# Gating in the projection's PSUM banks, pooling sums on VectorE, small copies on ScalarE in a two-layer decoder trunk

## The chip, the cores and the metric

The kernel runs on one core of a Trainium2 chip. Its engines are TensorE (PE in the profile, its weight loads apart as PEld), VectorE (DVE), ScalarE (ACT), GpSimd (POOL) and SyncE (SP), which issues the DMA transfers. The metric is the device time of one execution in microseconds; the median over runs counts.

## The reference

One sequence of 512 tokens with 1024 features goes through two layers, each `x <- x + RMSNorm_post(mixer(RMSNorm_pre(x)))`, all in float32. What the change touches lies in layer 0 and in the parameters of layer 1's state-space branch:

```python
def even_mixer(h, w_in, pool_w, pool_scale, w_out):        # layer 0
    z = h @ w_in                                           # 1024 x 3072
    q, k, v, ga, pu, gb = jnp.split(z, [A, 2*A, 3*A, 4*A, 4*A + POOL_WIDTH], axis=-1)   # A = 512
    q, k = rope_partial(q), rope_partial(k)
    att  = moba_attention(q, k, v) * jax.nn.silu(ga)       # 4 heads of 128
    pool = multiscale_pool(pu, pool_w, pool_scale) * jax.nn.silu(gb)   # windows 2, 4, 8, 16
    return jnp.concatenate([att, pool], axis=-1) @ w_out

def multiscale_pool(u, ...):    # group g: mean of the last w_g tokens, minus u, times pool_w[g]
```

Layer 1 does the same with a state-space branch (S5, which needs powers of a complex number per state) and a 31-tap convolution branch with gates.

## The kernel before

**Precision and weights.** A float32 product is made of three matmuls on a high and a low part: `mm3` (lines 104, 105, 106: high by high, then the two cross products). `split` (L107 to L111) makes the parts: ScalarE copies the source into the high part (`S.activation`, L109), and VectorE, or GpSimd where it is told to, subtracts it from the source (`tt`, L58). So all subtractions, additions and products show as L58, scaled ones as L61. Weights come in blocks of 256 rows: SP loads `raw` (three buffers, L146), ScalarE makes `whi` (L109, with a gain L169), and `wlo` is made by VectorE (L61, layer 0's input projection) or by GpSimd (L58, layer 0's output projection and layer 1). `whi` and `wlo` have four buffers each; a block's buffers come free when its last matmul or split is done.

**Stages of layer 0.** After the norm and transposes come the column groups of the input projection, each of four output tiles of 128x512 in the four PSUM banks of pool `pz` (tag `z`): q, k, v, then `pg0` and `pg1` (values and gates of pooling groups 0, 1 and 2, 3), then `ga` (gates of the four attention heads). Attention runs on TensorE between the matmuls of pg0 to ga: scores `s`, weights `P`, their transposes `tp` (L721), the split `ph`, `pl` and the sums `o`. Then the output projection (`out_mm`, order groups `o00` and `o01` for the two halves of the columns) makes eight tiles of 128 tokens by 512 columns; for each it goes through eight blocks of gated branch output, first the four pooling groups (`ch`, `cl`), then the four heads (also in a tile that the profile calls `qk`).

**Pooling.** `pool_branch` makes, for a group, the gate `sgb`, the padded values `u`, and one to four doubling sums `ub` (L802 and the line after it): each clears a strip at the left edge and adds a tile to itself, shifted. `m` (a `wt`) is the mean minus the value. `pool_mm` multiplies by `pool_w` and the gate and splits into `ch` and `cl`.

**Gating of the heads.** After `ga`, VectorE multiplies each of the four banks by `rbc` (the reciprocal norm, along the tokens) into an SBUF tile `sgs[g]`, ScalarE applies Silu in place, VectorE multiplies by the attention output `att` into another SBUF tile `yc`, and `split` makes the two parts. Each bank is free after its first product.

**Side work on GpSimd.** From about 30 to 164 us GpSimd computes for layer 1 the phasors (`U`, `pa`) and the tables (`tab`, two tiles per step, chains of short products on 128x4 to 128x256, stored by SP as `td`, L757). The table tiles share a ring of buffers (tag `ch`) with the pooling groups' `ch` and `cl`. `s5_bc` copies the powers `AR`, `AI` in reversed order into `GR`, `GI` (eight copies of 128x32, L537 and L538), from which VectorE makes `g` (L58).

**What sets the order.** The program is not run in the order of its text: the framework's scheduler simulates it and gives each engine a fixed list of instructions, which that engine executes strictly in order, waiting on semaphores. SP's DMA issues stand in such a list too. An instruction that waits holds back all that stand behind it on its engine.

Of the kernel before, what the change touches and what calls it, by code (L numbers as in the profile page):

```python
# [14 lines left out]
F32 = mybir.dt.float32  # L15
# [3 lines left out]
AF = mybir.ActivationFunctionType  # L19
# [4 lines left out]
MUL, ADD, SUB, MAX, MIN = ALU.mult, ALU.add, ALU.subtract, ALU.max, ALU.min  # L24
# [3 lines left out]
Q = 4  # L28
# [10 lines left out]
def tile_hybrid_trunk(ctx, tc, A):  # L39
    nc = tc.nc  # L40
    x, out = A["x"], A["out"]
    V, S, G = nc.vector, nc.scalar, nc.gpsimd
# [6 lines left out]
    pz = ctx.enter_context(tc.tile_pool(name="pz", bufs=4, space=PSUM))  # L49
# [4 lines left out]
    def f(ap):  # L54
        return ap.bitcast(F32)

    def tt(e, o, a, b, op):
        return e.tensor_tensor(o, a, b, op=op)  # L58
# [10 lines left out]
    def tcol(t):  # L69
        return slice(t * 128, (t + 1) * 128)  # L70
# [37 lines left out]
    def split(hi, lo, src, eng=None):  # L108
        i = S.activation(hi, src, AF.Copy)  # L109
        tt(eng or V, lo, src, f(hi), SUB)  # L110
        return i  # L111
# [85 lines left out]
    def proj_t(name, sh, sl):  # L197

        z = zbanks()
        for j in range(4):  # L200
            w = wblock(name, j)
            for t in range(4):
                for i in range(2):
                    k = j * 2 + i
                    last_mm[0] = mm3(z[t], sh[k][:, tcol(t)], sl[k][:, tcol(t)], w.h[i], w.l[i], k == 0, k == 7).ins
            run_after(name, j)
        return z
# [26 lines left out]
    ps = l0.enter_context(tc.tile_pool(name="ps", bufs=2, space=PSUM))  # L234
# [89 lines left out]
    def wt():  # L324
        return wk.tile([128, 512], F32, tag="t", name="wt", bufs=5)
# [39 lines left out]
    def e2k(tag, bufs=1):  # L365
        return pe.tile([128, 512], F32, tag=tag, name=tag, bufs=bufs)
# [136 lines left out]
    def s5_bc():  # L503
        AR, AI, fr, fi = (par[n] for n in ("AR", "AI", "fr", "fi"))
        ct1 = pe.tile([128, NG, NI], F32, name="ct1")
        ct2 = pe.tile([128, NG, NI], F32, name="ct2")
        p = pt.tile([128, 512], F32, tag="t", name="tp")
        with tc.issue_after(q_end[0]):
            for m in range(4):
                nc.tensor.transpose(p[:, tcol(m)], par["cn"][:, m].rearrange("p a b -> p (a b)"), ident)  # L510
        S.activation(ct1.rearrange("p g c -> p (g c)"), p, AF.Copy, scale=s2)
        S.activation(ct2[0:64].rearrange("p g c -> p (g c)"), p[64:128], AF.Copy)
        S.activation(ct2[64:128].rearrange("p g c -> p (g c)"), p[0:64], AF.Copy, scale=-1.0)
        for g, r in enumerate(DR):
            d = par["dm"][r, :, g * NI:g * NI + NI]
            tt(G, d, d, ident[r, r.start + NI:r.stop].unsqueeze(1).to_broadcast([32, NG // 2, NI]), MUL)
        IC = pe.tile([128, 8, 128 + 2 * NI], F32, name="IC")
        G.tensor_copy(IC[:, :, 0:128], ident.unsqueeze(1).to_broadcast([128, 8, 128]))
        kk = pe.tile([128, NG // 2, 2 * NI], F32, name="kk")


        b1, b2 = par["b1"], par["b2"]

        def bc(ap):
            return ap.unsqueeze(2).to_broadcast([128, NG, NI])
        u1, u2 = (e2k(n, b).rearrange("p (g i) -> p g i", i=NI) for n, b in (("e2", 1), ("pin", 2)))
        tt(V, u1, b2, bc(fi), MUL)
        tt(V, u2, b1, bc(fi), MUL)
        tt(V, b1, b1, bc(fr), MUL)
        tt(V, b2, b2, bc(fr), MUL)  # L530
        tt(V, b1, b1, u1, SUB)
        tt(V, b2, b2, u2, ADD)

        GR = pe.tile([128, Q, NG], F32, name="GR")
        GI = pe.tile([128, Q, NG], F32, name="GI")
        for i in range(Q):
            G.tensor_copy(GR[:, i], AR[:, Q - 1 - i])  # L537
            G.tensor_copy(GI[:, i], AI[:, Q - 1 - i])  # L538
        par.update(ct1=ct1, ct2=ct2, GR=GR, GI=GI, IC=IC, kk=kk)

    def s5_phasors():
# [93 lines left out]
    rbc = wk.tile([128, T], F32, name="rbc", bufs=1)  # L635
# [13 lines left out]
    def q_first():  # L649
        z = zbanks()  # L650
        steps = [("h", 0), ("w", 0), ("h", 1), (0, 0), ("h", 2), (1, 0), ("w", 1), (0, 1), (1, 1), "l", ("h", 3), (2, 0), ("w", 2), ("x", 0), ("x", 1), (2, 1), (3, 0), (3, 1), ("w", 3), ("x", 2), ("x", 3), "s", (0, 2), (1, 2), (2, 2), (3, 2), (0, 3), (1, 3), (2, 3), (3, 3)]
        w = {}
        for st in steps:
            if st == "l":
                s5_lam()
            elif st == "s":
                root0()
                run_after("q", 0)
            elif st[0] == "x":
                ss0(st[1])  # L660
            elif st[0] == "h":
                hT0(st[1])
            elif st[0] == "w":
                w[st[1]] = wblock("q", st[1], 0)
            else:
                t, j = st
                for i in range(2):
                    k = j * 2 + i
                    last_mm[0] = mm3(z[t], h0h[k][:, tcol(t)], h0l[k][:, tcol(t)], w[j].h[i], w[j].l[i], k == 0, k == 7).ins
        q_end[0] = last_mm[0]  # L670
        return z

    qk = []
    for name, nxt in (("q", "k"), ("k", "v")):
        z = q_first() if name == "q" else proj_t(name, h0h, h0l)
# [51 lines left out]
    att = []  # L727
# [36 lines left out]
    z = proj_t("v", h0h, h0l)  # L764
    for t in range(4):
        a = xv.tile([128, 512], F32R, tag="v", name="vh")
        b = xv.tile([128, 512], F32R, tag="v", name="vl")
# [19 lines left out]
    ch, cl = [None] * 8, [None] * 8  # L787
    ms, sgb = {}, {}

    def pool_branch(g, zg, zu):  # L790
        sgb[g] = pu.tile([128, 16 + 512], F32, tag="u", name="sgb", bufs=5)[:, 0:512]
        tt(V, sgb[g], zg, rbc, MUL)
        S.activation(sgb[g], sgb[g], AF.Silu)
        w = 2 << g
        u = pu.tile([128, 16 + 512], F32, tag="u", name="u", bufs=5)
        G.memset(u[:, 0:16], 0.0)
        tt(V, u[:, 16:], zu, rbc, MUL)
        a = u
        step = 1
        while step < w:  # L800
            b = pu.tile([128, 16 + 512], F32, tag="u", name="ub", bufs=5)
            G.memset(b[:, 0:step], 0.0)  # L802
            tt(G if g in (0, 1) else V, b[:, step:], a[:, step:], a[:, :528 - step], ADD)
            a = b
            step *= 2
        m = wt()
        tt(V, m[:, 0:16], a[:, 16:32], rcnt[:, g], MUL)
        tt(V, m[:, 0:16], m[:, 0:16], u[:, 16:32], SUB)
        stt(V, m[:, 16:], a[:, 32:], 1.0 / w, u[:, 32:], MUL, SUB)
        mh = cp.tile([128, 512], F32R, tag="mh", name="mh")  # L810
        ml = cp.tile([128, 512], F32R, tag="ml", name="ml")
        split(mh, ml, m)
        ms[g] = (mh, ml)
# [10 lines left out]
    for n, nxt in ((0, "pg1"), (1, "ga")):  # L824
        z = proj_c(f"pg{n}", h0h, h0l)
        for i in range(2):
            g = 2 * n + i
# [33 lines left out]
    after["ga", 2] += [load_gains]  # L861
    z = proj_c("ga", h0h, h0l)
    cah, cal = bigr(), bigr()
    sgs = [wt() for _ in range(4)]
    for g in range(4):
        tt(V, sgs[g], z[g], rbc, MUL)
        if g == 1:
            pool_mm(3)
        S.activation(sgs[g], sgs[g], AF.Silu)
    for g in range(4):  # L870
        sg = sgs[g]
        yc = wt()
        tt(V, yc, att[0][:, g], sg, MUL)
        ch[g], cl[g] = cah[:, g], cal[:, g]
        split(ch[g], cl[g], yc)


    def out_mm(z, names, c, t, ch, cl, kord, ahead):
# [39 lines left out]

    xns, yg, ss = [], defaultdict(list), defaultdict(list)
    for t, q in ((0, 0), (1, 0), (0, 1), (1, 1), (2, 0), (2, 1), (3, 0), (3, 1)):  # L920
        z = pz.tile([128, 512], F32, tag="z", name="z")
        out_mm(z, f"o0{q}", full, t, ch, cl, OK0, lambda j: 3 if t + q == 0 else 3 - j)
        ss[t].append(sumsq(z, wk))
        yg[t].append(wt())
        tt(V, yg[t][q], z, gpost[q], MUL)
        if (t, q) == (3, 0):
            prefetch(index["sa", 0] + 4)
        if q:
            if t:
                next_hT(t - 1, xns[t - 1])  # L930
            xns.append(add_norm(t, yg[t], ss[t]))
# [12 lines left out]
    ps = l1.enter_context(tc.tile_pool(name="ps1", bufs=1, space=PSUM))  # L944
# [220 lines left out]
    z = proj_c("sb", hh, hl)  # L1165
# [3 lines left out]
    z = proj_c("ab1", hh, hl)  # L1169
    for i in range(2):  # L1170
        conv_in(2 + i, z[i], z[2 + i])
    z = proj_c("gd", hh, hl)
# [8 lines left out]
    z = proj_c("gc", hh, hl)  # L1181
# [13 lines left out]
    ch, cl, sn = [], [], []  # L1195
# [12 lines left out]
    for n in range(2):  # L1208

        with tc.issue_after(ln["mu"]) if n else nullcontext():  # L1210
            z = proj_c(f"gl{n}", yh, yl, nk=4)
        for i in range(2):
            m = 2 * n + i
            s = ct()
            S.activation(s, z[2 + i], AF.Sigmoid, bias=gb[:, 4 + m:5 + m])
            a = ct()
# [5 lines left out]
    ch, cl = by_k((c1[0], c2[0])), by_k((c1[1], c2[1]))  # L1222
# [14 lines left out]
    for m in range(4):  # L1237
        z = (pt.tile([128, 512], F32, tag="t", name="z") if m % 2 else (ps, pa)[m // 2].tile([128, 512], F32, tag=("s", "acc")[m // 2], name="z"))
# [5 lines left out]
        a = ct()  # L1244
# [3 lines left out]
    z = zo  # L1248
# [5 lines left out]
    for t in range(4):  # L1254
# [4 lines left out]
        for c in cols:  # L1259
            z = pz.tile([128, 512], F32, tag="z", name="z")  # L1260
# [42 lines left out]
```

## Time and profile before

| | us |
|---|---|
| median of three runs (lowest, highest) | 463.68 (462.9, 465.01) |
| the profiled execution | 464.39 |
| its span, first to last instruction | 462.6 |
| TensorE busy | 442.1 (96%) |
| TensorE weight loads busy | 362.7 (78%) |
| VectorE busy | 344.2 (74%) |
| GpSimd busy | 251.4 (54%) |
| ScalarE busy | 243.9 (53%) |

The mean granted TensorE clock was 0.987 of full speed (the two levels are 2.4 GHz, written 1.00, and 1.2 GHz, written 0.50; a stretch that holds both shows a value between). A table of busy time by stretch says how much each engine worked there; in a line of the timeline the two numbers are start and duration, and a bracket gives the idle time of that engine before it and who ended it. TensorE is nearly always busy, so its few idle stretches and those at the lower clock are what the table has to be read for.

### The profile page before, as it was taken

The numbers are of one execution on the slowest core, as the hardware profiler recorded it, in microseconds if no ns is written. First come the engines' busy times: TensorE is split into PE (matmuls) and PEld (weight loads), VectorE is DVE, ScalarE is ACT, GpSimd is POOL, SyncE is SP. The second block draws the span as 40 slices with busy tenths as digits, with TensorE's granted clock in tenths as the row PEclk, the third lists the DMA queues.
The fourth block names the chain that finished last, engine by engine and source line by source line (L and its number), as shares of the span: only waits on it lengthen the run. The fifth ranks groups of instructions, "written<-read, shape, count | busy, mean of one in ns | idle before, by whom it ended". The sixth has DMA issues, their size and how long they took to land.

```text
span 462.6 us, 6753 instructions
## 1 busy us (share of the span) xinstructions
PE 442.1 (96%) x2185; PEld 362.7 (78%) x2185; DVE 344.2 (74%) x706; ACT 243.9 (53%) x445; POOL 251.4 (54%) x428
## 2 busy tenths in 40 slices
PE   7999989999999979889999999999999999999994
PEld 5788868888878858678879988877877877788884
DVE  3998698757677475864884579998998898656444
ACT  7655435635847334624764535649866326373431
POOL 1019994019999926650281576668997944430000
PEclk9999999999999979989999999999999999999999
DMA  7974064341332555350045693886343542122013
GB/s 255 236 135 162 25 217 147 114 126 47 132 96 77 136 181 195 118 165 1 1 139 156 184 264 103 240 219 161 93 123 113 150 136 92 47 92 91 0 70 112
DMA packets 62403, 59.58 MB, mean 129 GB/s; under 512 B 20537, under 2 KB 43713, under 8 KB 62368
## 3 DMA queue, kind: packets, MB, share of 16 engines
q1 hardware_dynamic: 62368, 59.16, 43.0%
q8 instruction: 17, 0.28, 0.2%
q14 instruction: 18, 0.15, 0.1%
HBM read 50.62 MB, written 8.52 MB: 128 GB/s over the span
## 4 chain that ended last, share of the span: by engine, by line
PE 66%; POOL 16%; DVE 10%; DMA 3%; issue 2%; ACT 1%; SPq 0%; DVEq 0%; POOLq 0%; ACTq 0%
PE z L105 19%; PE z L104 19%; PE z L106 19%; POOL tab L58 12%; PE s L1000 2%; DVE wt L58 1%; PE y L1035 1%; PE y L1032 1%; POOL U L58 1%; DMA ldt<-o_log_dt 1%; DVE wlo L61 1%; POOL pa L58 1%; DMA qk<-x 1%; DVE qk L58 1%; PE tp L589 1%
## 5 line engine op out<-in xcount | busy, mean ns | idle before, releaser
L58 POOL TENSOR_TENSOR wlo<-raw,whi 128x1024 fp32r<-128x1024 f32 (+2 forms) x50 | 88.4, 1790 | 71.8 <-ACT whi L109 71.8
L105 PE MATMUL z<-hl,whi 128*128 128x512 f32 (+1 forms) x288 | 106.6, 371 | 0.0
L104 PE MATMUL z<-hh,whi 128*128 128x512 f32 (+1 forms) x288 | 106.3, 375 | 0.0
L106 PE MATMUL z<-hh,wlo 128*128 128x512 f32 (+1 forms) x288 | 106.2, 371 | 0.0
L61 DVE SCALAR_TENSOR_TENSOR acc<-gp,dw,acc 128x512 f32<-128x512 f32 x100 | 75.1, 751 | 2.2
L109 ACT ACTIVATE whi<-raw 128x1024 fp32r<-128x1024 f32 (+2 forms) x54 | 45.3, 871 | 37.7 <-PE z L105 19.2
L104 PEld LDWEIGHTS z<-hh,whi 128*128 128x128 f32 x288 | 54.5, 190 | 9.7 <-issue 0.8
L106 PEld LDWEIGHTS z<-hh,wlo 128*128 128x128 f32 x288 | 54.6, 190 | 9.0 <-issue 0.2
L105 PEld LDWEIGHTS z<-hl,whi 128*128 128x128 f32 x288 | 54.8, 190 | 8.8 <-issue 0.3
L61 DVE SCALAR_TENSOR_TENSOR wlo<-raw,gcol,whi 128x512 fp32r<-128x512 f32 x48 | 36.6, 783 | 6.6 <-ACT whi L169 4.8
L169 ACT ACTIVATE whi<-raw,gcol 128x512 fp32r<-128x512 f32 x48 | 32.1, 715 | 15.6 <-PE z L106 7.5
L105 PE MATMUL z<-wlo,hh 128*128 128x512 f32 x96 | 38.3, 401 | 1.6 <-DVE wlo L61 1.5
L104 PE MATMUL z<-whi,hh 128*128 128x512 f32 x96 | 38.1, 405 | 1.1 <-ACT whi L169 1.1
L106 PE MATMUL z<-whi,hl 128*128 128x512 f32 x96 | 37.9, 398 | 0.0
L58 POOL TENSOR_TENSOR tab<-tab,U 128x4 f32<-128x4 f32 (+6 forms) x112 | 36.7, 361 | 0.0
L306 ACT ACTIVATE junk<-z 128x512 bf16<-128x512 f32 (+1 forms) x17 | 9.7, 570 | 30.4 <-PE z L106 30.3
L58 POOL TENSOR_TENSOR tab<-tab 128x4 f32<-128x4 f32 (+6 forms) x56 | 23.5, 439 | 0.0
L105 PEld LDWEIGHTS z<-wlo,hh 128*128 128x128 f32 x96 | 18.2, 189 | 6.2 <-DVE wlo L61 2.7
L104 PEld LDWEIGHTS z<-whi,hh 128*128 128x128 f32 x96 | 18.1, 191 | 5.6 <-ACT whi L169 1.8
L106 PEld LDWEIGHTS z<-whi,hl 128*128 128x128 f32 x96 | 18.2, 190 | 3.4
L58 POOL TENSOR_TENSOR pacc<-pacc,lt 128x512 f32<-128x512 f32 x14 | 18.9, 1354 | 0.2
L58 POOL TENSOR_TENSOR dm<-dm,ident 32x256 f32<-32x256 f32 x2 | 1.5, 750 | 30.8 <-DMA dm<-o_d 30.7
(325 smaller groups left out, 1008.3 us busy)
## 6 DMA issues: line engine op xcount, KB each, us to landing
raw<-e_w_in SPq DMA_DIRECT2D x15, 512.0 KB, 4.0
raw<-e_w_in SPq DMA_DIRECT2D x18, 256.0 KB, 3.6
raw<-e_w_out SPq DMA_DIRECT2D x8, 512.0 KB, 4.6
raw<-o_w_in SPq DMA_DIRECT2D x16, 256.0 KB, 3.5
rot<-td SPq DMA_DIRECT2D x16, 256.0 KB, 5.6
raw<-o_w_in SPq DMA_DIRECT2D x8, 512.0 KB, 3.9
raw<-o_w_out SPq DMA_DIRECT2D x8, 512.0 KB, 3.7
qk<-x SPq DMA_DIRECT2D x8, 256.0 KB, 4.1
```

Source lines behind the costliest of these rows:

```text
L58: return e.tensor_tensor(o, a, b, op=op)
L61: e.scalar_tensor_tensor(o, a, s, b, op0=op0, op1=op1)
L104: nc.tensor.matmul(p, sh, mh, start=start, stop=False)
L105: nc.tensor.matmul(p, sh, ml, start=False, stop=False)
L106: return nc.tensor.matmul(p, sl, mh, start=False, stop=stop)
L109: i = S.activation(hi, src, AF.Copy)
L169: S.activation(hi[:, h], b.raw[:, h], AF.Copy, scale=gc)
L306: S.activation(jk[:, 0:src.shape[-1]], src, AF.Square, scale=1.0 / 32.0, accum_out=ss)
L589: nc.tensor.matmul(p[:, i], ev[:, h + i], IC[:, c % 2 * 4 + h + i], start=True, stop=True)
L1000: nc.tensor.matmul(s[:, i], sets[m][0][hf, i], Ut[m][hf, i], start=True, stop=True)
L1032: nc.tensor.matmul(y[:, r], tb[:, m * 4 + r], Ut[m][:, r], start=True, stop=False)
L1035: nc.tensor.matmul(y[i * 64:i * 64 + 64, r], gt[:, g], xf[i][:, r], start=False, stop=True)
```

## The change

Four edits. The eight copies into `GR` and `GI` go from GpSimd to ScalarE. In `pool_branch` all clearings (four of `u`, ten of `ub`) and the three sums of groups 0 and 1 go from GpSimd to VectorE, where the sums of groups 2 and 3 were already. The gated heads are computed in place in the four PSUM banks of `ga`, so that both products and Silu read and write the bank, and `split` reads it. Two of the output projection's tiles, (0,0) and (1,0), take banks of the scores' pool `ps` (tag `s`, two banks, also used by pooling's `y`) in place of `pz`.

```diff
@@ s5_bc
         for i in range(Q):
-            G.tensor_copy(GR[:, i], AR[:, Q - 1 - i])
-            G.tensor_copy(GI[:, i], AI[:, Q - 1 - i])
+            S.activation(GR[:, i], AR[:, Q - 1 - i], AF.Copy)
+            S.activation(GI[:, i], AI[:, Q - 1 - i], AF.Copy)
@@ pool_branch
-        G.memset(u[:, 0:16], 0.0)
+        V.memset(u[:, 0:16], 0.0)
         tt(V, u[:, 16:], zu, rbc, MUL)
...
-            G.memset(b[:, 0:step], 0.0)
-            tt(G if g in (0, 1) else V, b[:, step:], a[:, step:], a[:, :528 - step], ADD)
+            V.memset(b[:, 0:step], 0.0)
+            tt(V, b[:, step:], a[:, step:], a[:, :528 - step], ADD)
@@ after the projection ga
-    sgs = [wt() for _ in range(4)]
+
     for g in range(4):
-        tt(V, sgs[g], z[g], rbc, MUL)
+        tt(V, z[g], z[g], rbc, MUL)
         if g == 1:
             pool_mm(3)
-        S.activation(sgs[g], sgs[g], AF.Silu)
+        S.activation(z[g], z[g], AF.Silu)
     for g in range(4):
-        sg = sgs[g]
-        yc = wt()
-        tt(V, yc, att[0][:, g], sg, MUL)
+        tt(V, z[g], z[g], att[0][:, g], MUL)
         ch[g], cl[g] = cah[:, g], cal[:, g]
-        split(ch[g], cl[g], yc)
+        split(ch[g], cl[g], z[g])
@@ output projection of layer 0
     for t, q in ((0, 0), (1, 0), (0, 1), (1, 1), (2, 0), (2, 1), (3, 0), (3, 1)):
-        z = pz.tile([128, 512], F32, tag="z", name="z")
+        z = (ps if t < 2 and not q else pz).tile([128, 512], F32, tag="s" if t < 2 and not q else "z", name="z")
```

The scheduler makes new lists from it. The first place is VectorE in the second half of pooling, around the sum for group 2. Numbers in the names tell buffers apart: `ub_2186` and `ub_2189` are sums of this group, `pl_2075` is a low part of attention weights, `cl_2010` a low part of pooling group 0. Before:

```order
L61 SCALAR_TENSOR_TENSOR wt_2007<-y_2003,pscale_1576,sgb_1930 128x512 [waits PE_49]
L58 TENSOR_TENSOR ml_1964<-wt_1959,mh_1963 128x512 [waits Activation_49]
L58 TENSOR_TENSOR ub_2186<-ub_2183 128x526 [waits DVE_49,Pool_49]
L58 TENSOR_TENSOR cl_2010<-wt_2007,ch_2009 128x512 [waits DMAHW6_49,Activation_49]
L58 TENSOR_TENSOR ub_2189<-ub_2186 128x524 [waits DVE_49,Pool_49]
L58 TENSOR_TENSOR pl_2075<-tp_2069,ph_2074 128x512 [waits Activation_49]
```

And of the change:

```order
L61 SCALAR_TENSOR_TENSOR wt_2007<-y_2003,pscale_1576,sgb_1930 128x512 [waits PE_49]
L58 TENSOR_TENSOR ml_1964<-wt_1959,mh_1963 128x512 [waits Activation_49]
L802 MEMSET ub_2186 128x2 [waits DVE_49]
L58 TENSOR_TENSOR ub_2186<-ub_2183 128x526
L58 TENSOR_TENSOR cl_2010<-wt_2007,ch_2009 128x512 [waits DMAHW6_49,Activation_49,Pool_49]
L802 MEMSET ub_2189 128x4 [waits DVE_49]
L58 TENSOR_TENSOR ub_2189<-ub_2186 128x524
L58 TENSOR_TENSOR pl_2075<-tp_2069,ph_2074 128x512 [waits Activation_49]
```

The two clearings stand in VectorE's own list now; the sums no longer wait for GpSimd, and `cl_2010`, whose buffer was a table tile, now does.

The second place is VectorE after `ga`. `z_2229` to `z_2232` are the four banks, `qk_1623` the attention output, `qk_2384` and `qk_2385` the high and low parts of the gated heads, `cl_2400` (before) and `cl_2396` (now) the low part of pooling group 3. Before:

```order
L58 TENSOR_TENSOR wt_2388<-z_2231,rbc_149 128x512 [waits DVE_49]
L58 TENSOR_TENSOR wt_2389<-z_2232,rbc_149 128x512 [waits DVE_49]
L58 TENSOR_TENSOR cl_2400<-wt_2397,ch_2399 128x512 [waits DMAHW1_49,Activation_49]
L58 TENSOR_TENSOR wt_2408<-qk_1623,wt_2386 128x512 [waits DVE_49]
L58 TENSOR_TENSOR wt_2412<-qk_1623,wt_2387 128x512 [waits DVE_49]
L58 TENSOR_TENSOR qk_2385<-wt_2408,qk_2384 128x512 [waits Activation_49]
L58 TENSOR_TENSOR wt_2416<-qk_1623,wt_2388 128x512 [waits DVE_49]
L58 TENSOR_TENSOR wt_2420<-qk_1623,wt_2389 128x512 [waits DVE_49]
L58 TENSOR_TENSOR qk_2385<-wt_2412,qk_2384 128x512 [waits Activation_49]
L58 TENSOR_TENSOR qk_2385<-wt_2416,qk_2384 128x512 [waits Activation_49]
```

And of the change:

```order
L58 TENSOR_TENSOR z_2229<-z_2229,qk_1623 128x512 [waits Activation_49]
L58 TENSOR_TENSOR z_2231<-z_2231,rbc_149 128x512 [waits PE_49]
L58 TENSOR_TENSOR z_2230<-z_2230,qk_1623 128x512 [waits Activation_49]
L58 TENSOR_TENSOR qk_2385<-z_2229,qk_2384 128x512 [waits Activation_49]
L58 TENSOR_TENSOR z_2232<-z_2232,rbc_149 128x512 [waits PE_49]
L61 SCALAR_TENSOR_TENSOR wt_2393<-y_2389,pscale_1576,sgb_2200 128x512 [waits PE_49]
L58 TENSOR_TENSOR z_2231<-z_2231,qk_1623 128x512 [waits Activation_49]
L58 TENSOR_TENSOR qk_2385<-z_2230,qk_2384 128x512 [waits Activation_49]
L58 TENSOR_TENSOR z_2232<-z_2232,qk_1623 128x512 [waits Activation_49]
L58 TENSOR_TENSOR cl_2396<-wt_2393,ch_2395 128x512 [waits DMAHW7_49,DMAHW2_49,Activation_49]
```

Of the eight operations that made and split the gated heads from two SBUF tiles none is left with two SBUF operands; `cl_2396` is the one row here that still has them.

The third place is TensorE at the start of the output projection. `z_2444`, `z_2497` (before) and `z_2436`, `z_2489` (now) are the tiles (0,0) and (1,0); `z_2519` is tile (0,1), which takes a bank of `ga`; `qk_2449` is the first weight block of `o01`. Before, where the heads' rows begin:

```order
L104 MATMUL z_2444<-whi_2354,qk_2384 128x512 [waits Activation_49]
L105 MATMUL z_2444<-wlo_2355,qk_2384 128x512 [waits Pool_49]
L104 MATMUL z_2497<-whi_2354,qk_2384 128x512
L105 MATMUL z_2497<-wlo_2355,qk_2384 128x512
L106 MATMUL z_2444<-whi_2354,qk_2385 128x512 [waits DVE_49]
L106 MATMUL z_2497<-whi_2354,qk_2385 128x512
L104 MATMUL z_2527<-qk_2457,ch_2009 128x512 [waits Activation_49]
```

And of the change, from the tenth matmul of the output projection on:

```order
L104 MATMUL z_2519<-qk_2449,ch_2009 128x512 [waits DVE_49,Activation_49]
L104 MATMUL z_2489<-whi_2280,ch_2009 128x512 [waits DVE_49]
L105 MATMUL z_2489<-wlo_2281,ch_2009 128x512
...
L106 MATMUL z_2489<-whi_2310,cl_2272 128x512
L105 MATMUL z_2519<-qk_2449,ch_2009 128x512 [waits Pool_49]
L106 MATMUL z_2519<-qk_2449,cl_2010 128x512
```

The heads' rows come later (27 matmuls after the first row shown instead of none), and a matmul that needs a bank of `ga` and the first block of `o01` now stands tenth in line.

## Rows read from the trace of the kernel before

**Rows 1.** Waits of TensorE: who for whom, us in total, times, longest.

```profile
PE tp L721 <- DVE pl L58: 3.3, 1, 3.3
PE z L106 <- DVE qk L58: 3.2, 1, 3.2
...
PE s L104 <- ACT P L712: 1.0, 1, 1.0
```

**Rows 2.** Stretches: width; PE, PEld, DVE, ACT, POOL busy; clock, DMA share, GB/s.

```profile
40.00:50.00 10.00, 10.00 (x48) 8.28 (x47) 4.83 (x16) 4.31 (x8) 9.33 (x42) 1.00 0.26 84
...
58.00:66.00 8.00, 6.33 (x28) 4.08 (x27) 8.00 (x20) 3.27 (x7) 7.50 (x21) 1.00 0.72 220
118.00:156.00 38.00, 37.04 (x184) 30.81 (x183) 28.94 (x70) 23.78 (x46) 37.80 (x110) 1.00 0.39 119
165.30:170.30 5.00, 5.00 (x14) 4.12 (x15) 4.46 (x10) 3.39 (x6) 0.31 (x3) 0.50 0.62 177
...
197.90:201.40 3.50, 3.47 (x8) 2.74 (x9) 3.50 (x2) 1.15 (x2) 3.50 (x2) 0.52 0.56 156
```

**Rows 3.** Timeline of the first stall (start, duration; idle before and its releaser).

```profile
155.48 0.74 DVE L58 TENSOR_TENSOR cl<-wt,ch 128x512 fp32r<-128x512 f32 x1
...
162.39 1.44 POOL L58 TENSOR_TENSOR tab<-tab 128x256 f32<-128x256 f32 x2
...
163.74 0.17 POOL L802 MEMSET ub<- 128x2 f32 x2
163.90 0.70 DVE L58 TENSOR_TENSOR ub<-ub 128x524 f32<-128x524 f32 x1 [7.68 <-POOL ub L802]
...
165.26 0.94 PE L721 MATMUL tp<-ident,P 128*128 128x128 f32 x3 [3.32 <-DVE pl L58]
```

**Rows 4.** Timeline of the second stall.

```profile
181.59 0.38 SPq L146 DMA_DIRECT2D raw<-e_w_out  x1
...
185.28 0.39 PE L106 MATMUL z<-hh,wlo 128*128 128x512 f32 x1
...
185.51 0.39 PE L104 MATMUL y<-mh,pwh 128*128 128x512 f32 x1
...
192.00 8.11 POOL L58 TENSOR_TENSOR qk<-raw,qk 128x1024 fp32r<-128x1024 f32 x3 [2.97 <-ACT qk L109]
...
195.04 7.31 DVE L58 TENSOR_TENSOR qk<-wt,qk 128x512 fp32r<-128x512 f32 x3
...
197.93 0.73 PE L106 MATMUL z<-whi,qk 128*128 128x512 f32 x1 [3.17 <-DVE qk L58]
```

**Rows 5.** VectorE by form, 180 to 200 us (count, busy us, mean ns, idle before).

```profile
L58 DVE TENSOR_TENSOR qk<-wt,qk 128x512 fp32r<-128x512 f32 x3 | 6.3, 2129 | 0.0
L58 DVE TENSOR_TENSOR wt<-qk,wt 128x512 f32<-128x512 f32 x4 | 4.9, 1242 | 0.1
L58 DVE TENSOR_TENSOR wt<-z,rbc 128x512 f32<-128x512 f32 x4 | 2.7, 686 | 3.4 <-PE z L106 3.4
```

**Rows 6.** Timeline of VectorE, 40 to 50 us.

```profile
49.98 1.35 DVE L58 TENSOR_TENSOR g<-GR,ct 128x512 f32<-128x512 f32 x2 [5.07 <-POOL GR L537]
```

**Rows 7.** VectorE by form, 118 to 172 us.

```profile
L58 DVE TENSOR_TENSOR ub<-u 128x527 f32<-128x527 f32 x2 | 1.4, 691 | 0.0
```

**Rows 8.** GpSimd by form, the same stretch.

```profile
L58 POOL TENSOR_TENSOR tab<-tab 128x256 f32<-128x256 f32 x6 | 4.7, 809 | 0.0
...
L58 POOL TENSOR_TENSOR ub<-u 128x527 f32<-128x527 f32 x2 | 2.5, 1266 | 0.0
...
L796 POOL MEMSET u<- 128x16 f32 x4 | 0.4, 112 | 3.1 <-DVE wt L58 3.1
```

**Rows 9.** DMA issues, 145 to 206 us: KB each, median us to landing.

```profile
raw<-e_w_out SPq DMA_DIRECT2D x7, 512.0 KB, 5.1
```

**Rows 10.** ScalarE by form, 180 to 200 us.

```profile
L109 ACT ACTIVATE qk<-raw 128x1024 fp32r<-128x1024 f32 x3 | 3.0, 1041 | 0.0
L869 ACT ACTIVATE wt<-wt 128x512 f32<-128x512 f32 x4 | 2.5, 632 | 2.4 <-DVE wt L58 2.4
```

**Rows 11.** ScalarE by form, whole span: a small copy.

```profile
L591 ACT ACTIVATE kk<-tp 128x64 f32<-128x64 f32 x8 | 1.8, 228 | 0.0
```

## Prediction

> **What bounds the kernel now.** I read first who waits for whom on TensorE, since TensorE is busy 96% of the span and only what makes it wait or run slowly can be won. Two single waits of over 3 us stand out: transposes of attention weights that wait for VectorE's `pl`, and matmuls that wait for its `qk`; another, of scores for ScalarE's `P`, is 1.0 us [rows 1]. Then the stretches: those behind the two waits show what a wait costs beyond itself. Behind the first TensorE is busy for 5.0 us at a granted clock of 0.50, behind the second for 3.5 us at 0.52 [rows 2]. That is the lower level, 1.2 GHz, and each matmul takes twice the time there, so half of such a stretch is lost too. Then the timelines of the two.
>
> *First stall.* VectorE ends `cl` at 156.2 and then does nothing for 7.68 us. It waits for a clearing of `ub`, 128x2 and 128x4, which stands in GpSimd's list behind the tables: the last table products end at 163.8, the clearings of 0.17 us follow, and at 163.90 VectorE goes on. Behind that sum in VectorE's list stands `pl`, which TensorE needs: it is idle 3.32 us until 165.26 [rows 3]. Loss: 3.3 + 5.0 x 0.5 = 5.8 us.
>
> *Second stall.* After `ga` the heads are gated. From 192.0 to 200.1 GpSimd splits three weight blocks (8.11 us, 2.7 each), and at 195.04 three VectorE splits of 128x512 take 7.31 us; TensorE is idle 3.17 us until 197.93 [rows 4]. The means by form tell which operations suffer: those with two SBUF operands, 2129 and 1242 ns in this stretch; those that read a PSUM bank and one SBUF tile, of the same size, 686 ns [rows 5]. The split at the end of the row of three took as long as a GpSimd operation each. So it is the pairing of two SBUF operands with a long GpSimd operation that costs, by these rows. Loss: 3.2 + 3.5 x 0.48 = 4.9 us.
>
> *Two small ones.* At 58 to 66 us TensorE is busy 6.33 of 8.00 us, VectorE all 8.00 [rows 2]: it works off a backlog, since it had waited 5.07 us for GpSimd's last copy into `GR`, which ended at 50.0 [rows 6]. Loss up to 1.7 us, no lower clock. And the 1.0 us for `P` I lay to VectorE's waits for GpSimd's pooling sums, which stand ahead of the scaling of `P` in its list. All four together: 5.8 + 4.9 + 1.7 + 1.0 = 13.4 us.
>
> **The change part by part.** *Clearings and sums on VectorE.* VectorE gains 3 sums at 0.69 us [rows 7] and 14 clearings. A clearing on VectorE of this size is not in the trace; on GpSimd one takes 0.11 [rows 8]. From below: nothing added beyond 0.05; from above one table operation's 0.81 each, if each had to wait for GpSimd. I take 0.11, the row of the same operation: 3 x 0.69 + 14 x 0.11 = 3.6 us. The cover is VectorE's idle time in 118 to 156, 38.00 - 28.94 = 9.1 us, besides the 7.7 that goes [rows 2, 3]. At the upper end, 3 x (0.69 + 0.81) + 14 x 0.81 = 15.8 us stand against 9.1 + 7.7 = 16.8, so even that just fits, though not each piece of it.
>
> GpSimd loses three sums of up to 1.27 and 14 clearings of 0.11, 5.3 us, most of it ahead of the last table [rows 8]; so the tables end 4 to 5 us sooner, at 159 to 160. But VectorE no longer waits for their end: after `cl` come a clearing, a sum (0.70) and `pl` (0.68 or less), so `pl` is done by about 156.2 + 1.5 + up to 2 us that the added work shifts, under 160; TensorE asks at 161.9. The whole first stall goes: 5.8 us. What is late next in VectorE's list is nothing that I can find before 172.
>
> GpSimd's sums of 1.27 us, for which VectorE waited, go as well; of the 1.0 us for `P` I take 0.7, between 0 and 1.0. Here a rule of the Trainium skill speaks against the change. Rows first: `ub` sums on VectorE with two SBUF operands took 0.69 us [rows 7] while GpSimd was busy 37.80 of 38.00 us [rows 2]; so beside short table operations they pay nearly nothing. The GPSIMD Engine Reference (sections "Key points" and 1) says that GpSimd shares its SBUF interfaces with VectorE and contends with VectorE instructions that have two SBUF inputs; by it each moved sum would pay up to a table operation, the 0.7 would be 0, and the forecast 0.7 us later. Rows 5 agree with the rule beside long operations, rows 7 don't beside short ones.
>
> *Gating in PSUM.* The four Silu and eight VectorE operations stay, but none of the eight keeps two SBUF operands: each goes to about 0.69 us [rows 5], so VectorE needs 12 x 0.69 = 8.3 us from the first finished bank on and is not held by GpSimd. Removed: 3 x (2.13 - 0.69) + 4 x (1.24 - 0.69) = 6.5 us of VectorE time. In exchange the banks are held until the fourth operation, and TensorE's list changes: nine matmuls of tile (0,0), then one of tile (0,1) that needs the first bank and the first block of `o01`. Let E = 185.5, the end of `ga`. TensorE does 3 matmuls of `y` and 9 more, 0.23 us from start to start [rows 4], and is there at E + 2.8. That block's load is issued at 181.59 [rows 4] and lands 5.1 us later [rows 9], at E + 1.2; ScalarE's copy takes 1.04 [rows 10]: E + 2.2. So it is in time by 0.6. GpSimd's low part, 2.7, ends at E + 4.9, and TensorE asks at E + 5.1: in time by 0.2. Then `cl` of pooling group 3, the one operation left with two SBUF operands: ScalarE has before it two Silu, three copies of 0.6 and two blocks of 1.04, so `ch` is made at about E + 6.5 to 7; `cl` ends at E + 8, or E + 10.7 behind a GpSimd operation of 2.7; TensorE asks at 36 x 0.23 + 0.7 = E + 9.0. So what remains is 0 to 1.7 us of waiting, on margins of 0.2 to 1 us. I take 1.0, and with it no lower clock, as after the waits of under 1 us at 58 to 66. Gain: 4.9 - 1.0 = 3.9. Bounds: 4.9, and 0 if a wait as long as the old one comes back.
>
> *Banks of `ps` for two tiles.* They cost nothing themselves; without them (0,0) would wait for the gating. The scores and `y` that used these banks are done by E + 0.7, except that tile (1,0) waits for VectorE to read `y`, about 0.7, so by E + 1.5 or a little later; TensorE asks at E + 3.1.
>
> *Copies on ScalarE.* 8 x 0.23 [rows 11] = 1.8 us, bounded by 0 and by 8 x 1.04 = 8.3, the longest copy here. ScalarE is busy 4.31 of the 10.00 us from 40 to 50 [rows 2], which covers 5.7 of that, and in its list all eight stand ahead of the first copy into `ct`, which `g` needs too. So `g` can start when `ct` is there, by an estimate most of the 5.07 us sooner, and the backlog at 58 to 66 is smaller by that. Of the 1.7 us I take 1.2; bounds 0 (transfers bind instead: DMA share 0.72 there [rows 2]) and 1.7.
>
> *Sum.* 5.8 + 3.9 + 1.2 + 0.7 = 11.6 us against the profiled execution's 464.39: 452.8. That execution is 0.71 above the median of the runs, so 452.1, forecast 452.0. Layer 1 has the same lists but for single rows, and TensorE is full there, so the gain should reach the end.
>
> **The rivals.** *B, a new wait takes the place of the second stall.* For: the margins of 0.2 and 0.6 us; ScalarE's list puts the loads of `o01` ahead of two Silu, so a late transfer holds the heads too. Against: nothing but those margins. The price is a wait of 3 us and its lower clock, the 4.9 of now: 452.0 + 3.9 = 455.9, to 457.
>
> *C, the first stall comes back through the shared ring.* `cl` of group 0 now waits for GpSimd and for the store of a table. If it is the last table: tables end at 160, the store lands some 5 us later, as the loads do [rows 9], `pl` 2 us behind at 167: TensorE waits 5 us and loses 2.5 more. 452.0 + 7.5 = 459.5. Against: the buffers go round, and the table of this one should be two steps earlier, done some 20 us before.
>
> *D, slower: the bank in the tenth place.* TensorE's list is in order, so if the load of `o01`'s first block is late, all stands still though nine more matmuls are ready. A slip by one GpSimd split and one transfer is 2.7 + 5.1 = 7.8 us, less the margin of 0.6 and with 2.5 of lower clock 9.7: 452.0 + 8.7 = 460.7. Two such rounds: 17.5, so 468.5, slower. It decides from a wait of about 12 us on (gains elsewhere 7.7, the old stall's 4.9, less 2.5 for the clock, 2.3 for half a per cent). Against: the load's issue is tied to GpSimd's splits, which the change only makes earlier.
>
> *E, no change:* the waits go and TensorE idles elsewhere for as long, on transfers. For: the DMA share of 0.72 at 58 to 66. Against: in the stretches behind both long stalls it is about 0.6, and TensorE waited for VectorE there. About 463.
>
> **How the numbers follow.** Forecast 0.62 (its own range 449.5 to 454.5: all of 13.4 is 450.3, less a little for waits that no row names; and another 2 us of waits upward), B 0.20, C 0.08, D 0.04 and E 0.06. Half a per cent, 2.3 us, is about what a measurement can tell from no change. Faster 0.62 + 0.20 + 0.08 = 0.90, same 0.06, slower 0.04. The range, 449 to 459, takes in B and most of the way to C.
>
> **What would show it.** Right: no idle time of VectorE of over 2 us at 156 to 164, and no clock under 0.9 at 160 to 175; the four splits of heads at about 0.69 us; TensorE busy over 7 of 8 us at 58 to 66; `g` before 47 us. Wrong: TensorE waiting over 3 us after the first ten matmuls of the output projection (B, D) or on `pl` (C), or new waits on TensorE behind VectorE's clearings.

## The result and the profile after

The changed kernel took 452.84 us in the median, before 464.35: ratio 0.9728, interval 0.9671 to 0.9786. Forecast were 452.0 and a range of 449 to 459. One of the four executions behind that median took 461.1 us, the others 451.3 to 454.2. The one of 461.1 was the first to be profiled: it held a 5.2 us wait in layer 1 that the two later profiles of this kernel don't have; so the rows here are of one of those, 452.16 us with a span of 450.4, against 464.39 and 462.6 before: 12.2 us less. On two more occasions the kernel's ratio was 0.9757 (0.9709 to 0.9806) and 0.9739 (0.9713 to 0.9765).

The waits of TensorE, longest first (who for whom, us in total, times, longest):

```profile
PE z L104 <- ACT qk L109: 2.1, 1, 2.1
PE tp L330 <- POOL ident masks.py:199: 1.4, 1, 1.4
PE z L104 <- ACT whi L169: 1.0, 1, 1.0
```

The two waits of over 3 us and the one for `P` [rows 1] are gone. On top stands a new one, for a weight block that ScalarE copies (`qk<-raw`). The stretches (width; PE, PEld, DVE, ACT, POOL busy; clock, DMA share, GB/s):

```profile
58.00:66.00 8.00, 8.00 (x41) 6.63 (x40) 7.93 (x23) 2.43 (x5) 7.50 (x25) 1.00 0.65 211
118.00:156.00 38.00, 38.00 (x190) 31.78 (x189) 34.52 (x85) 24.56 (x46) 38.00 (x97) 1.00 0.29 90
...
170.00:180.00 10.00, 8.15 (x36) 6.33 (x34) 5.14 (x8) 2.96 (x6) 3.86 (x2) 1.00 1.00 375
...
181.00:184.20 3.20, 3.20 (x10) 2.46 (x9) 1.70 (x3) 3.20 (x6) 3.20 (x2) 0.51 0.05 13
```

At 58 to 66 us TensorE does 41 matmuls where it did 28 [rows 2]; at 118 to 156 it is never idle, and VectorE carries 5.6 us more. Of the two stretches at the lower clock in [rows 2] one is left, 3.2 us at 0.51, now behind the new wait; the row above it shows a DMA share of 1.00 just before.

VectorE at the place of the first stall:

```profile
150.10 0.73 DVE L58 TENSOR_TENSOR ub<-ub 128x526 f32<-128x526 f32 x1
150.12 0.06 DVE L802 MEMSET ub<- 128x2 f32 x1
150.75 0.72 DVE L58 TENSOR_TENSOR cl<-wt,ch 128x512 fp32r<-128x512 f32 x1
151.41 0.73 DVE L58 TENSOR_TENSOR ub<-ub 128x524 f32<-128x524 f32 x1
151.43 0.06 DVE L802 MEMSET ub<- 128x4 f32 x1
152.06 0.69 DVE L58 TENSOR_TENSOR pl<-tp,ph 128x512 fp32r<-128x512 f32 x1
```

It goes from `cl` to the sum and to `pl` without a gap, where it had waited 7.68 us [rows 3]. Then the gating, VectorE by form, 168 to 192 us (count, busy us, mean ns, idle before):

```profile
L58 DVE TENSOR_TENSOR z<-z,rbc 128x512 f32<-128x512 f32 x4 | 2.8, 697 | 3.6 <-PE z L106 3.6
L58 DVE TENSOR_TENSOR z<-z,qk 128x512 f32<-128x512 f32 x4 | 2.8, 694 | 4.3 <-ACT z L869 4.3
L58 DVE TENSOR_TENSOR qk<-z,qk 128x512 fp32r<-128x512 f32 x4 | 2.6, 681 | 0.8 <-ACT qk L109 0.8
```

All twelve take 0.7 us; the splits had 2129 ns [rows 5]. And the new wait, in the timeline:

```profile
172.03 0.38 SPq L146 DMA_DIRECT2D raw<-e_w_out  x1
...
179.16 1.06 ACT L109 ACTIVATE qk<-raw 128x1024 fp32r<-128x1024 f32 x1 [4.56 <-DMA raw<-e_w_out]
180.27 0.50 PE L104 MATMUL z<-qk,ch 128*128 128x512 f32 x1 [2.13 <-ACT qk L109]
```

The load of the first block of `o01` is issued at 172.03 and has landed at 179.16, when ScalarE starts to copy it, 7.1 us later; the tenth matmul of the output projection stands behind it and everything after that matmul too.

Matmuls that both kernels have show where the time came from (start in us):

| matmul | before | after | gained so far |
|---|---|---|---|
| first transpose `tp` L683 at 61 us | 61.53 | 61.02 | 0.5 |
| first score `s` | 80.00 | 77.26 | 2.7 |
| first `y` of pooling | 152.55 | 147.85 | 4.7 |
| transposes of `dwn` L848, in `ga` | 179.58 | 169.26 | 10.3 |
| `z<-whi,c1h` that waits for `ct` | 404.81 | 392.62 | 12.2 |

So: 0.5 up to 61 us, 2.2 behind the copies, 2.0 in pooling, 5.6 at the first stall, 1.9 from `ga` on. The 0.5 is the start, which differs between executions: that first row lies between 60.75 and 62.52 over all profiles, whatever the edits.

### The profile page after: what moved, and what is told of

It reads as the page before. It is cut to its first block, busy times and chain, and to the rows that moved or that the text cites. A ratio compares the mean times of both kernels' runs of the same rounds, so it can differ in the third digit from the quotient of the medians.

```text
span 459.3 us, 6743 instructions
## 1 busy us (share of the span) xinstructions
PE 439.1 (96%) x2185; PEld 362.5 (79%) x2185; DVE 351.6 (77%) x723; ACT 245.1 (53%) x453; POOL 251.4 (55%) x403
## 4 chain that ended last, share of the span: by engine, by line
PE 71%; DVE 14%; DMA 5%; ACT 3%; issue 3%; POOL 2%; SPq 1%; DVEq 0%; POOLq 0%; ACTq 0%
PE z L104 21%; PE z L105 20%; PE z L106 20%; DVE acc L61 9%; DMA raw<-e_w_out 1%; DMA xh<-x 1%; ACT whi L109 1%; PE tp L321 1%; POOL wlo L58 1%; PE tp L721 1%; PE tp L589 1%; DMA raw<-e_w_in 1%; DMA yb<-yd 1%; PE s L998 1%; DVE s L58 1%
## 5 line engine op out<-in xcount | busy, mean ns | idle before, releaser
L58 POOL TENSOR_TENSOR tab<-tab,U 128x4 f32<-128x4 f32 (+6 forms) x112 | 41.3, 399 | 0.0
L105 PEld LDWEIGHTS z<-wlo,hh 128*128 128x128 f32 x96 | 18.5, 192 | 3.6
L58 POOL TENSOR_TENSOR rw<-rw,rot 128x512 f32<-128x512 f32 x8 | 10.4, 1297 | 14.4 <-ACT rw L1016 14.4
```

What stands on the lines that cost most here:

```text
L105: nc.tensor.matmul(p, sh, ml, start=False, stop=False)
```

## Experiments

All times are medians; ratios are against the kernel before on the same chip.

**The changed kernel again.**

> The changed kernel once more, for an undisturbed profile. Theory: the first stall is gone (granted clock over 0.9 at 160 to 175 us, VectorE idle less than 2 us before the pl of that place), the k stage too; what is left at the start of the output projection is a wait of 0 to 3.5 us of TensorE for the first block of o01, and its length follows the landing of that block's load. Time 451 to 453 us. Rival: that wait is the same in every execution, 3 us and more with a stretch at the lower clock behind it; then the time is 453 to 455 and two thirds of the second stall is lost again.

454.91 us (0.9757), in the rival's range and above the theory's. Its profile is the one above: wait of 2.1 us, then 3.2 us at half clock, 3.7 us in all; in the 461.1 us execution the same wait was 3.4, again with a stretch at the lower clock, and in a third profile (`after3` below, 451.51 us) it was 2.6 with the clock at 1.00 behind it. So the wait is there in every profile of this kernel, as the rival has it, but with a length that differs: it gives back 2.6 us or more of the 4.9 that the second stall had cost.

**Edit 2 alone.** Clearings and sums of pooling on VectorE, nothing else.

> The kernel before with the second edit alone (clearings and sums of pooling on VectorE). Theory: the first stall of 5.8 us and most of the 1.0 us wait for P go, the k stage and the second stall stay: 464.4 - 6.5 = 457.9, 457 to 459. Rival: the sums and clearings cost VectorE and the stall only moves on to the next thing in its list; then 461 or more.

459.85 us, ratio 0.9878 (0.9835 to 0.9922). It lies between theory and rival: the first stall is gone, but less was won than its 5.8 us and the wait for `P`. The trace shows where the rest went: from the transposes of `dwn` to the wait for `ct` (the last two rows of the table above) it takes 229.0 us where the kernel before took 225.2, with new waits of 1.0 and 0.7 us ahead of the second stall and 6.8 us at the lower clock behind it (before 3.4).

**The clearings alone.**

```diff
-            tt(V, b[:, step:], a[:, step:], a[:, :528 - step], ADD)      # as in the change
+            tt(G if g in (0, 1) else V, b[:, step:], a[:, step:], a[:, :528 - step], ADD)
```

(and the other three edits undone)

> The kernel before with only the 14 clearings on VectorE; the three sums of groups 0 and 1 stay on GpSimd. Theory: the first stall was a clearing queued behind the tables, so it goes (5.8 us), and the 1.0 us for P stays: 458 to 459.5, as far as the second edit as a whole. Rival: the stall comes from the tables' length, to which the sums on GpSimd add 3.6 us; then VectorE still waits over 3 us for GpSimd near 160 us and the time is over 461.

457.71 us, ratio 0.9864 (0.983 to 0.9898). Its VectorE, and what GpSimd and SP do at that time:

```profile
155.25 0.73 DVE L58 TENSOR_TENSOR cl<-wt,ch 128x512 fp32r<-128x512 f32 x1
155.92 0.74 DVE L58 TENSOR_TENSOR ub<-ub 128x524 f32<-128x524 f32 x1
...
156.58 1.14 DVE L58 TENSOR_TENSOR pl<-tp,ph 128x512 fp32r<-128x512 f32 x2
...
163.52 2.35 POOL L58 TENSOR_TENSOR tab<-tab 128x256 f32<-128x256 f32 x2
...
164.75 1.47 SPq L757 DMA_DIRECT2D td<-tab  x2
```

The tables end no sooner than before (stored at 164.75, before at 163.18), and yet `pl` starts at 156.58 and not at 164.52. So the stall was the clearing's place in GpSimd's list: with the tables as long as before it is gone. Two clearings, 0.17 us together, had cost about 6 (6.3 by the ratio; forecast for the stall was 5.8).

**Edit 1 alone.** The eight copies on ScalarE.

> The kernel before with the first edit alone (eight small copies on ScalarE). Theory: VectorE's first g comes 4 to 5 us sooner, TensorE's idle time at 58 to 66 us (1.7) falls under 0.6: 463.2, 462.5 to 464. Rival: the loads of weights bind there, nothing moves: 464.4, same.

462.27 us, ratio 0.9945 (0.9912 to 0.9977): a gain of 2.8 us by the medians, of 2.6 by the ratio, more than the 1.2 forecast. The stretch shows it whole:

```profile
58.00:66.00 8.00, 8.00 (x41) 6.66 (x40) 7.96 (x23) 2.51 (x5) 7.50 (x23) 1.00 0.69 218
118.00:156.00 38.00, 34.01 (x154) 28.08 (x154) 31.35 (x59) 19.49 (x38) 35.64 (x110) 0.91 0.30 98
```

41 matmuls and not 28, with the DMA share at 0.69, as high as before; transfers did not bind. The second row warns against reading the profile's total: this execution (465.81, nine of the twelve 460.9 to 463.5) lost 4 us in pooling.

**Edits 3 and 4 alone.** Gating in PSUM and the two other banks.

> The kernel before with the third and fourth edit alone (gating in the PSUM banks, two tiles in the other pool). Theory: the second stall of 4.9 us goes but for 1.0, the first stays: 460.5, 459 to 462. Rival: the wait for the first block of o01 eats what was won, since a load lands as late here as in the changed kernel; then 463 to 465.

459.25 us, ratio 0.9868 (0.9823 to 0.9913): 6.1 us by the ratio where 3.9 was forecast. Its profile (an execution of 466.68 us, with a wait of 6.8 us in layer 1) has neither the second stall nor a wait at the tenth matmul: so alone this edit won the whole second stall. That the gain is over the stall's 4.9 us may be the clock: in this profile it did not fall behind the first stall, and the stretch from the first `y` to the transposes of `dwn` took 24.6 us where the kernel before took 27.0. Here the first stall still holds TensorE back. The last of the eight loads of x is out by 174.2 us, the load of the first block of `o01` is issued 7.6 us later, at 181.85, and has landed at 185.54, after 3.7 us. The sum of the three parts alone, 1.22 + 0.55 + 1.32 = 3.1%, is more than the 2.4 to 2.7% that the change as a whole gave; the new wait of the whole change is the difference that its traces show.

**Edit 3 without edit 4.** All eight output tiles in the pool `z`.

```diff
-        z = (ps if t < 2 and not q else pz).tile([128, 512], F32, tag="s" if t < 2 and not q else "z", name="z")
+        z = pz.tile([128, 512], F32, tag="z", name="z")
```

> The kernel before with the gating in the PSUM banks alone; the two first output tiles stay in the pool z. Theory: the first tile needs the first bank, freed by its split only after Silu, two products and the copy, some 3 to 4 us after its last matmul, so TensorE waits 0 to 2 us at the start of the output projection; part of the second stall's 4.9 us is lost again: 459 to 463 beside the 459.3 of gating with the fourth edit. Rival: the bank is free in time, since the first head is finished by the projection's end; then within 0.5% of 459.3, and the fourth edit is worth nothing.

460.53 us, ratio 0.9927 (0.9904 to 0.995), and in its timeline of TensorE:

```profile
190.57 0.50 PE L104 MATMUL z<-whi,ch 128*128 128x512 f32 x1 [1.30 <-DVE qk L58]
195.59 0.50 PE L106 MATMUL z<-whi,cl 128*128 128x512 f32 x1 [1.73 <-DVE cl L58]
```

The first is the bank: the second split must be done before the second tile can begin. The other is the `cl` with two SBUF operands, which took 2.90 us there. The times alone don't decide: the two medians differ by 0.3%, the ratios by 0.6%, and their intervals overlap a little. The 1.30 us wait is what speaks against the rival, so the fourth edit probably pays.

**The gated head through SBUF, split from there.**

```diff
+        yc = wt()
-        tt(V, z[g], z[g], att[0][:, g], MUL)
+        tt(V, yc, z[g], att[0][:, g], MUL)
-        split(ch[g], cl[g], z[g])
+        split(ch[g], cl[g], yc)
```

> The changed kernel, but the gated head is written to an SBUF tile and split from there, so that each of the four splits again has two SBUF operands (the product still reads the bank); the scheduler here puts the first matmul of o01 13 places later. Theory: beside GpSimd's splits of 2.4 to 2.7 us each such VectorE split takes 1.3 to 2.5 us again, TensorE waits 1 to 3 us for them in place of the tenth-matmul wait, and the time is 452 to 455, no better than the changed kernel. Rival: two SBUF operands cost nothing by themselves, and the second stall was only the late order of the operations; then the splits take 0.7 us and, with the tenth-matmul wait gone, 449.5 to 451.

453.54 us, ratio 0.9767 (0.9733 to 0.9801), as the theory has it. Since TensorE's list changed too, the length of the splits tells more than the time. VectorE by form, 180 to 193 us, and GpSimd's timeline:

```profile
L58 DVE TENSOR_TENSOR qk<-wt,qk 128x512 fp32r<-128x512 f32 x4 | 9.1, 2323 | 0.0
L58 DVE TENSOR_TENSOR cl<-wt,ch 128x512 fp32r<-128x512 f32 x1 | 1.9, 1904 | 0.0
L58 DVE TENSOR_TENSOR wt<-z,qk 128x512 f32<-128x512 f32 x2 | 1.4, 686 | 0.7 <-ACT z L868 0.7
```

```profile
183.38 8.37 POOL L58 TENSOR_TENSOR qk<-raw,qk 128x1024 fp32r<-128x1024 f32 x3 [0.62 <-ACT qk L109]
```

The same split that takes 681 ns from a bank takes 2323 from SBUF, nearly one GpSimd operation each (8.37 / 3 = 2.8), while the product beside it, with one operand in PSUM, stays at 686; one of the two ran inside a GpSimd split. TensorE waits 1.8 us for a split again. This is the cause of the second stall, shown with one operand moved. It is what the Trainium skill says in the GPSIMD Engine Reference, "Key points": GpSimd shares its SBUF interfaces with VectorE, "contention with DVE instructions in a 2-port perf mode or with two SBUF inputs".

**The loads of x behind the output weights.**

```diff
-    for t in range(4):
-        load_x(xt[t], t)
...
         out_mm(z, f"o0{q}", full, t, ch, cl, OK0, lambda j: 3 if t + q == 0 else 3 - j)
+        if t + q == 0:
+            with tc.issue_after(ld_ins[0].ins):
+                for t_ in range(4):
+                    load_x(xt[t_], t_)
```

> The changed kernel, with its eight loads of x for the residual (256 KB each) issued behind the output projection's weights and not ahead of the first block of o01. Theory: TensorE's 2.1 to 3.4 us wait at the tenth matmul of the output projection comes from that block's load, which takes 7 us and not 5 because the eight loads run beside it (DMA share 1.00 there); here the load lands in about 5 us, the wait is under 0.5 us, the clock stays at 1.00 at 175 to 190 us, and the time is 3 us below the changed kernel's: 449.5 to 451. Rival: the load is late because its buffer comes free late (GpSimd's split of the second block at 169), and not because of the other transfers; then the wait stays over 1.5 us and the time within 1 us of the changed kernel's.

448.88 us, ratio 0.9673 (0.9636 to 0.971), under the 449.5 that was the lower end of the theory. Its six executions lie within 1.5 us; of the changed kernel's six on the first repeat five went from 452.2 to 455.5, one was at 464.6. The load and its user, and the stretch:

```profile
172.69 0.38 SPq L146 DMA_DIRECT2D raw<-e_w_out  x1
...
176.43 1.06 ACT L109 ACTIVATE qk<-raw 128x1024 fp32r<-128x1024 f32 x1 [1.19 <-DMA raw<-e_w_out]
```

```profile
170.00:180.00 10.00, 10.00 (x47) 8.19 (x47) 6.38 (x10) 6.06 (x10) 7.20 (x4) 1.00 0.60 195
```

3.7 us from issue to use and not 7.1, 195 GB/s and not 375, no wait there, no lower clock. The load is issued no sooner than in the changed kernel, so its buffer was not the reason; it was the company of the eight transfers that made it late.

**The sums back on GpSimd,** in the changed kernel and in the one with late loads; and those two beside them.

> The changed kernel, but the three sums of groups 0 and 1 stay on GpSimd (clearings on VectorE). In its list for SP the third block of output weights stands ahead of the last table stores; in the changed kernel behind them. Theory: the sums' move won at most the 0.7 us of the wait for P, and it put that load behind the tables; without it the tenth-matmul wait is shorter, under 1.5 us, and the time is the changed kernel's or up to 2 us less: 450 to 453. Rival: the sums on GpSimd hold VectorE and the tables, and the time is 2 us or more above the changed kernel's.

> The same, with the eight loads of x behind the output weights as well. Theory: with the crowding gone the place of the third block decides little; 448.5 to 450, as with the late loads alone, or 0.7 us more for the wait for P. Rival: both help separately, and it is 1 us or more faster than the late loads alone.

> The changed kernel beside these two on the same chip: 451 to 455, spread over several us from execution to execution, since the landing of the first block of o01 decides the tenth-matmul wait.

> The changed kernel with the late loads of x, beside the same: 448.5 to 450, and less spread than the changed kernel.

| | sums on VectorE | sums on GpSimd |
|---|---|---|
| loads of x early | 452.11, 0.9739 (0.9713 to 0.9765) | 450.72, 0.9702 (0.9678 to 0.9727) |
| loads of x late | 448.87, 0.9663 (0.9638 to 0.9689) | 450.06, 0.9694 (0.9669 to 0.9719) |

With the sums on VectorE the late loads win 3.2 us, clear of both intervals. With early loads the sums on VectorE are 1.4 us worse, with late loads 1.2 better; here the intervals overlap, so each alone is only likely. The profiles agree with the sign: with the sums on GpSimd and early loads the first `y` comes at 150.66, 2.5 us later than on VectorE beside it (148.12), but there is no wait at the tenth matmul. There the third block's load stands ahead of the last table stores, all loads of x are out by 169.3 us, and the load of `o01`'s first block, issued at 174.2, lands in 4.2 us. One expectation missed: the late loads spread over 2.5 us here, the changed kernel beside them over 1.6. The best median of the eleven kernels, late loads with all four edits, is 3.4% under the kernel before.

**The same distances in all fourteen traces.** Three stretches of TensorE's timeline, in us, tell the edits apart, since each is nearly the same in every run that has the edit:

| from, to | edit | runs without it | runs with it |
|---|---|---|---|
| first `tp` L683, first `s` | copies on ScalarE | 18.4 to 18.5 (five) | 16.2 (nine) |
| first `s`, first `y` | sums on VectorE | 72.4 to 73.2 (six; `copy` 77.7) | 70.6 (seven) |
| first `y`, transposes of `dwn` | clearings on VectorE | 24.6 to 27.0 (four) | 20.9 (three), 21.4 with the sums too (seven) |

So what was won in pooling comes from the sums and not from the clearings, and at the first stall the sums cost 0.5 us.

## Why the prediction was right, step by step

The time was right to 0.8 us, and its sum of 11.6 us to 0.6 (12.2 measured). Its terms were not; that the sum came out so close is in part luck, since one term was put 2.0 us too high and two others 2.3 too low:

| term | forecast | measured |
|---|---|---|
| first stall | 5.8 | 5.6 |
| second stall, less the new wait | 3.9 | 1.9 |
| copies, 58 to 66 us | 1.2 | 2.2 |
| pooling, wait for `P` | 0.7 | 2.0 |
| up to 61 us (the start) | 0 | 0.5 |

The signs that it named for being right all came: no idle time of VectorE over 0.1 us at 156 to 164, clock 1.00 at 160 to 175, the splits of heads at 0.68 us, 8.00 us busy at 58 to 66, `g` at 44.9 us. Its sign for B, a wait of over 3 us behind the first matmuls of the output projection, came in one profile of three.

*First stall.* As forecast, in cause too: a clearing queued behind tables, shown by the clearings alone. VectorE's idle time covered the added work but for 0.5 us. One step failed without harm here: the tables were to end 4 to 5 us sooner and ended 1.1 sooner (162.7, before 163.8). GpSimd did lose the sums and clearings, but its 176 operations into `tab` took 70.2 us together where they had taken 65.8; over all runs they took 69.9 to 70.9 with the sums on VectorE and 60.7 to 67.3 with them on GpSimd. So most of what the move saved GpSimd was lost again in its tables; no run isolates why.

*Second stall.* The mechanism held (gating alone, and the split from SBUF), the term did not. The step that failed is "That block's load ... lands 5.1 us later, at E + 1.2". It landed 7.1 us after its issue, and was issued 3.2 us before E and not 3.9, so it landed at about E + 4; so rival B came true in part, 3.7 us of wait and clock where 1.0 was put (in `after3`, without the lower clock, the term comes out at 2.9 and not 1.9). I had taken the median landing from a stretch in which the eight loads of x were long over when this block was loaded. TensorE came 10 us sooner, but the loads of x start when the tables' last stores are out of SP's list, and these moved by 1.6 us (163.18 to 161.58); so what had run one after the other now ran together. The wait that I weighed in VectorE's list, `cl`, was 0.3 us in the kernel with late loads.

*Copies.* The window's busy time gave 1.7 us of idle time; the count of matmuls in the same window, 28 before and 41 after, says 13 / 41 x 8 = 2.5. The profile models when matmuls end, so short waits between them probably count as busy. The upper bound was set too low: 1.7, measured 2.2.

*Pooling.* I counted TensorE's one wait of 1.0 us; 2.0 came, and the sums' move brought it in every run that has it. In 118 to 156 us TensorE did 190 matmuls where it did 184 [rows 2], which points the same way. The wait for `P` is not the whole of it: it was 0.4, 0.4 and 1.0 us in the three runs with the clearings on VectorE and the sums on GpSimd, and none of these gained clearly from the first `s` to the first `y`.

*The rule of the Trainium skill on shared interfaces.* Against the moved sums it would have cost the 0.7 us. The three moved sums took 0.70 to 0.82 us beside a GpSimd that was busy all the time, little over the 0.69 that was put. Later, beside the tables' longest products, two other sums took 1.1 (the clearing beside a sum took 0.06). So by these runs VectorE pays by the length of the GpSimd operation under way. That GpSimd's tables ran longer fits the rule from the other side, which the prediction did not weigh. Its row for a cheap sum, 0.69 [rows 7], was also weaker than it read it: one of the two sums behind that mean ran at 169.4 us, after the tables.

*Rivals.* C did not come: `cl` of group 0 waited for no table. D would have needed 12 us at the tenth matmul; the place was right, and the price was 2.1 to 3.4 us of wait. E did not come: what TensorE waited for a transfer took back a part of the gain only.

## What to carry to other kernels

A trivial operation on an engine with a long list can be worth more than a large one: look at what stands ahead of it, not at its length. In these runs work went well side by side on VectorE and GpSimd where VectorE had an operand in PSUM, or where GpSimd's operations were short; two SBUF operands beside a long GpSimd operation cost up to that operation's length. And after a stage is sped up, ask of every load in it what it now runs beside: a landing time measured in the slow kernel is a property of its neighbours, and an in-order list passes the lateness on to all that was ready.

## What was not expected of the hardware

A VectorE operation of 128x16 with two SBUF operands (`wt<-ub,rcnt`) took 2.26 us when it met a GpSimd operation of 2.81, as in this pair of the changed kernel:

```profile
162.72 2.81 POOL L58 TENSOR_TENSOR wlo<-raw,whi 128x1024 fp32r<-128x1024 f32 x1
163.31 2.26 DVE L58 TENSOR_TENSOR wt<-ub,rcnt 128x16 f32<-128x16 f32 x1
```

Both end within 0.04 us of each other, as does a pair in the kernel before (2.38 us beside 2.64): it looks like waiting for the end of the operation, not like sharing. And a clearing on VectorE costs 0.06 us, about half of GpSimd's 0.11 [rows 8].
